# Extra ones products on TensorE in the first stage of a hybrid decoder block

## The chip, the cores and the metric

The kernel runs on one core of a Trainium2 chip. The metric is the time of one execution on the device in microseconds (us); a smaller time is better. Durations of single instructions come from one profiled execution of the program.

## The reference

One decoder layer over 1024 tokens of width 1024, all in float32. A conditioning vector `c` is turned into six modulation rows of 1024 (shift, scale and gate for each of two sub-layers):

```python
cond = jax.nn.silu(c)
mod = (cond @ w_ada[l] + b_ada[l]).astype(x.dtype)
sh_a, sc_a, gt_a, sh_m, sc_m, gt_m = [m[:, None, :] for m in jnp.split(mod, N_MOD, axis=-1)]
h = rms_norm(x, g_attn_pre[l]) * (1 + sc_a) + sh_a
proj = h @ w_in[l]
...
mixed = jnp.concatenate([rms_norm(oa, g_mix_a[l]), rms_norm(ob, g_mix_b[l])], axis=-1)
y = mixed @ w_out[l]
x = x + gt_a * rms_norm(y, g_attn_post[l])
h = rms_norm(x, g_mlp_pre[l]) * (1 + sc_m) + sh_m
y = jnp.square(jax.nn.relu(h @ w_up[l])) @ w_down[l]
x = x + gt_m * rms_norm(y, g_mlp_post[l])
```

`oa` is sliding-window attention with sinks over 8 heads, `ob` a mixture of dilated windows over 8 heads. Only the first lines, down to `proj`, matter for this change: the first two rows of `mod` must be known before the first projection can start.

## The kernel before

**Stages.** The program first loads `x` in eight blocks of 128 tokens (`x_sb`, tb 0 to 7) and the two needed thirds of `w_ada` in eight chunks (`wa`, k 0 to 7; each holds, for 128 output columns of the shift and 128 of the scale, all 1024 rows as 128 partitions by 8). Then come the input projection and attention, the output projection, and an MLP that takes most of the span. Float32 products are made of float32r pairs: a matrix is split into a high and a low part (`hw` for the activations, `w_hl` for the weights), and three products (lines 771, 772, 774) stand for one.

**The first stage.** For a block tb, ScalarE squares and sums (L553), VectorE and GpSimd make the root (L409, L412), VectorE scales the block (L558) and TensorE transposes it in two groups of four 128x128 transposes (L568) into PSUM tiles `pxt`, of which there are two. For tb 0 to 4 ScalarE copies them to `xnT` (L573). For tb 5 to 7 the copy out of PSUM also applies scale and shift (L580 on ScalarE or L583 on VectorE), and L593 and L596 split the block.

For a chunk k of `wa`, the product with `cond` is shared between two engines. TensorE takes the first two of the eight rows in one-column products (L615, the step `mod`; for k = 0 it takes all eight, 16 products); VectorE takes the other six: L626, then five times L628, into `acc_a`. VectorE adds TensorE's part to `bb` (L620) in between. A second pair of one-column products with `ones` (L635, the step `misc`) sums `acc_a` over the partitions into `pm`, and VectorE makes from that `g_a` and `s_a` of chunk k (L640, L641). Then ScalarE modulates chunk k of `xnT` (L645) and makes the high part (L651), GpSimd the low part (L654), and TensorE multiplies it with the k-th slice of the first weight unit: ten products of 384 columns for the five blocks (L771, L772), and later five more with the low part (L774). `w_hl` is made by L473 on ScalarE and L478 on GpSimd. The sums of the five blocks stand in five PSUM tiles `acc` of 512 columns, of which the products use 384. After the last chunk each block's `acc` is read out (`evac`: rotation L700 to L704, values L684 and L689, queries and keys L711 to L717), and the projection of block 5 (the same lines 771 to 774, with `pj` as output) waits for one of those tiles.

A product of float32 operands, such as L615 and L635, stands in the trace as two rows of TensorE; the transposes and the float32r products as one.

**What sets the order.** A planner in the program (`Sched`) has an estimated duration for every step and a clock for every engine, and writes the instructions out in the order in which the steps would start by these estimates. Each engine then executes its instructions strictly in that order; a wait in one holds up all that stand behind it. Steps of TensorE stand in streams (`xt` for the transposes, `mod`, `misc`, `dense` for the products, and others); steps of L580/L583, L593 and L596 may go to one of two engines, whichever the planner expects to end first.

Of the kernel before, what the change touches and what calls it, by code (L numbers as in the profile page):

```python
# [19 lines left out]
P = 128  # L20
# [114 lines left out]
class Sched:  # L135


    def __init__(self):
        self.clk = dict(PE=0.0, ACT=0.0, DVE=0.0, POOL=0.0, SP=0.0)
        self.queue = {e: [] for e in ("ACT", "DVE", "POOL", "SP")}  # L140
        self.pe = {}
        self.launch = []
        self.seq = 0
        self.dma = 0.0

    def step(self, dur, emit, deps=(), takes=(), gives=(), prio=5, after=None, kind=""):
# [83 lines left out]
    def run(self, prefer):  # L230
        while True:
# [28 lines left out]
            e, s, o, name = best  # L260
            if e == "PE":
                self.pe[name].pop(0)
            elif o.alts:
# [40 lines left out]
def hybrid_block(ctx: ExitStack, tc: tile.TileContext, x, positions, w_ada, b_ada, g_attn_post, w_in, w_out,  # L304
# [193 lines left out]

    e_init = op("DVE", 0.3, lambda: (V.memset(ones[:], 1.0), V.memset(nhalf[:], -0.5)), prio=0)
    e = op("ACT", 0.1, lambda: A.activation(cond[:], c_raw, AF.Exp, scale=-1.0), [e_c], prio=0)  # L500
# [49 lines left out]
    def x_block(tb):  # L550
# [13 lines left out]
        for g in range(2):  # L564
            def tr(g=g):
                box[g] = pt.tile([P, 4, P], F32, name="pxt", tag="t")
                for k in range(4):
                    T.transpose(box[g][:, k], x_t[tb][:, (4 * g + k) * P:(4 * g + k + 1) * P], ident)  # L568
            d = pe_op("xt", 0.7, tr, [e], takes=[(r_t, 1)], gives=[(r_x_, 1)] if g and tb < FIRST else [])
            d_all.append(d)  # L570
# [34 lines left out]
    def mod_chunk(k):  # L605
# [170 lines left out]
    def tick():  # L776
        st.d += 1 / (TB * KC)

    def first_unit():
        accs = {}  # L780
        for k in range(KC):
            for part in range(2):
                for tb in range(FIRST):
                    pl, tag, r = acc_at[tb]

                    def emit(k=k, part=part, tb=tb, pl=pl, tag=tag):
                        if k == 0 and part == 0:
                            accs[tb] = pl.tile([P, 512], F32, name="acc", tag=tag)
                        proj_mm(accs[tb][:, :UW], k, w_hl[0, k], tb, part)
                    d = dense(0.322 if part == 0 else 0.161, emit, [w_e[0, k], e_hl[k] if part else e_hh[k]],  # L790
                              takes=[(r, 1)] if k == 0 and part == 0 else [],
                              after=tick if part else None)
# [1157 lines left out]
```

## Time and profile before

| | |
|---|---|
| median of 3 runs | 1197.91 us (1197.79 to 1198.57) |
| profiled execution, its own time | 1197.14 us |
| its span | 1195.4 us |
| instructions | 17424 |
| TensorE busy in the span | 96% |
| VectorE, ScalarE, GpSimd busy | 74%, 56%, 22% |
| mean granted TensorE clock | 0.988 |

The profile is one execution on the chip. Its rows name the line of the kernel, the engine (PE is TensorE's products, PEld its weight loads, DVE VectorE, ACT ScalarE, POOL GpSimd, SP the engine that issues DMAs), the tile written and the tiles read. In the timeline, adjacent rows of one kind are merged: the first number is the start in us from the span's start, the second the time from the first start to the last end, `x8` the count, and in brackets stands the idle time ahead of it and what ended that. A busy TensorE can be one at half clock.

### The profile page before, as it was taken

How to read it: one execution, taken by the hardware profiler on the slowest of the kernel's cores; microseconds unless marked ns; L12 is line 12 of the kernel's file. 1: busy time of each engine (PE TensorE's matmuls, PEld its weight loads, DVE VectorE, ACT ScalarE, POOL GpSimd, SP SyncE). 2: the span in 40 equal slices, each digit the busy share in tenths (PEclk: the TensorE clock that was granted, in tenths of full speed). 3: DMA queues.
4: the chain of work that ended last, by engine and by line, in shares of the span. 5: the costliest groups of instructions: out<-in, count | busy, mean ns of one | idle time of the engine just before them, and what ended most of it. 6: DMA issues, size and time to landing. Idle time of an engine off the chain costs nothing.

```text
span 1195.4 us, 17424 instructions
## 1 busy us (share of the span) xinstructions
PE 1143.5 (96%) x6064; PEld 998.0 (83%) x6064; DVE 881.3 (74%) x1794; ACT 666.6 (56%) x1411; POOL 264.6 (22%) x325
## 2 busy tenths in 40 slices
PE   7879999999998998999899999999999999999996
PEld 6869999989998896888688888888888888888885
DVE  4977667666789897667888955479763797646998
ACT  6457666556666787667657533473325643246542
POOL 6534655465655333111100000000000000000002
PEclk9889999999999999999999999999999999999999
DMA  9621333213231422555296126952268511586103
GB/s 290 189 60 60 89 98 97 77 52 102 76 87 54 125 53 77 179 201 204 113 381 246 36 73 238 340 168 62 81 218 284 191 36 53 179 287 220 36 19 141
DMA packets 104423, 166.53 MB, mean 139 GB/s; under 512 B 11152, under 2 KB 56336, under 8 KB 104336
## 3 DMA queue, kind: packets, MB, share of 16 engines
q1 hardware_dynamic: 104336, 165.42, 41.8%
q8 instruction: 48, 0.79, 0.3%
q14 instruction: 39, 0.32, 0.1%
HBM read 137.08 MB, written 28.31 MB: 138 GB/s over the span
## 4 chain that ended last, share of the span: by engine, by line
PE 76%; DVE 13%; issue 4%; ACT 3%; POOL 3%; DMA 1%; SPq 0%; DVEq 0%; POOLq 0%; ACTq 0%
PE mlp_ps L1773 16%; PE mlp_ps L1774 16%; PE mlp_ps L1772 16%; PE pj L771 4%; PE pj L774 3%; PE pj L772 3%; PE s_ps L997 3%; PE o_ps L1131 1%; PE pt_ps L1100 1%; DVE acc_a L628 1%; PE y_ps L1348 1%; PE y_ps L1350 1%; PE pm L615 1%; PE y_ps L1349 1%; PE pt_ps L1103 1%
## 5 line engine op out<-in xcount | busy, mean ns | idle before, releaser
L1772 PE MATMUL mlp_ps<-hw 128*128 128x512 f32 x896 | 350.4, 391 | 0.4 <-ACT hw L1534 0.4
L1773 PE MATMUL mlp_ps<-hw 128*128 128x512 f32 x896 | 349.2, 390 | 1.1 <-DVE hw L1540 1.1
L1774 PE MATMUL mlp_ps<-hw 128*128 128x512 f32 x896 | 349.1, 390 | 0.0
L1773 PEld LDWEIGHTS mlp_ps<-hw 128*128 128x128 f32 x896 | 168.6, 188 | 36.9 <-DVE hw L1540 1.4
L1772 PEld LDWEIGHTS mlp_ps<-hw 128*128 128x128 f32 x896 | 168.6, 188 | 36.1 <-ACT hw L1534 0.8
L1774 PEld LDWEIGHTS mlp_ps<-hw 128*128 128x128 f32 x896 | 168.5, 188 | 35.1
L1543 DVE TENSOR_TENSOR hw<-w,hw 128x1024 fp32r<-128x1024 f32 x96 | 114.6, 1219 | 93.5 <-ACT hw L1536 93.3
L1536 ACT CAST hw<-w 128x1024 fp32r<-128x1024 f32 x96 | 97.4, 1046 | 129.9 <-PE mlp_ps L1774 93.2
L1872 POOL TENSOR_TENSOR st<-st,nhalf 128x1 f32<-128x1 f32 x8 | 7.8, 978 | 602.8 <-DVE st L1870 602.8
L771 PE MATMUL pj<-w_hl,hw 128*128 128x384 f32 x344 | 128.2, 373 | 10.0 <-DVE sk L717 10.0
L774 PE MATMUL pj<-w_hl,hw 128*128 128x384 f32 x344 | 117.4, 341 | 0.0
L772 PE MATMUL pj<-w_hl,hw 128*128 128x384 f32 x344 | 117.1, 341 | 0.0
L1536 ACT CAST hw<-u 128x1024 fp32r<-128x1024 f32 x48 | 48.6, 1051 | 64.6 <-PE mlp_ps L1774 64.6
L1118 DVE TENSOR_TENSOR ph<-pt_ps,ph 128x512 fp32r<-128x512 f32 (+1 forms) x110 | 68.8, 643 | 18.5 <-ACT ph L1114 17.6
L771 PEld LDWEIGHTS pj<-w_hl,hw 128*128 128x128 f32 x344 | 65.8, 191 | 11.8 <-issue 8.7
L1543 DVE TENSOR_TENSOR hw<-u,hw 128x1024 fp32r<-128x1024 f32 x48 | 57.0, 1217 | 18.2 <-ACT hw L1536 18.2
L1114 ACT CAST ph<-pt_ps 128x512 fp32r<-128x512 f32 (+1 forms) x110 | 59.2, 560 | 13.8 <-PE pt_ps L1103 9.8
L772 PEld LDWEIGHTS pj<-w_hl,hw 128*128 128x128 f32 x344 | 66.2, 192 | 0.8 <-issue 0.2
L774 PEld LDWEIGHTS pj<-w_hl,hw 128*128 128x128 f32 x344 | 65.7, 191 | 0.0
L1027 POOL TENSOR_SCALAR p_sb<-p_sb,den 128x128 f32<-128x128 f32 (+3 forms) x64 | 50.1, 786 | 70.2 <-DVE den L1025 46.8
L1830 DVE TENSOR_TENSOR yacc<-yacc,mlp_ps 128x512 f32<-128x512 f32 x96 | 62.1, 680 | 3.3 <-PE mlp_ps L1774 3.3
L1022 ACT ACTIVATE p_sb<-p_sb,mn 128x128 f32<-128x128 f32 (+3 forms) x64 | 49.9, 780 | 20.4 <-DVE mn L1015 16.6
(209 smaller groups left out, 2202.6 us busy)
## 6 DMA issues: line engine op xcount, KB each, us to landing
hw<-s_dram SPq DMA_DIRECT2D x84, 512.0 KB, 4.5
wa_st<-in_w_ada SPq DMA_DIRECT2D x32, 512.0 KB, 4.0
w<-in_w_up SPq DMA_DIRECT2D x32, 512.0 KB, 5.4
w<-in_w_down SPq DMA_DIRECT2D x32, 512.0 KB, 8.0
s_dram<-hw SPq DMA_DIRECT2D x28, 512.0 KB, 4.3
x_sb<-in_x SPq DMA_DIRECT2D x16, 512.0 KB, 6.2
wa<-in_w_ada SPq DMA_DIRECT2D x16, 512.0 KB, 7.0
w_st<-in_w_in SPq DMA_DIRECT2D x32, 192.0 KB, 4.7
```

The costliest lines, as they stand in the source:

```text
L771: T.matmul(ps, hw[:, tb, 0, t], w[:, 0], start=(k == 0), stop=False)
L772: T.matmul(ps, hw[:, tb, 0, t], w[:, 1], start=False, stop=False)
L774: T.matmul(ps, hw[:, tb, 1, t], w[:, 0], start=False, stop=(k == KC - 1))
L1027: lambda b=b, qi=qi: G.tensor_scalar(rec.p[qi], rec.p[qi], b["den"][:], 1.0, ALU.mult, ALU.mult), [e], prio=1))
L1114: A.copy(b["ph"][:, 0, :w], b["pt"][:, :w])
L1118: V.tensor_tensor(b["ph"][:, 1, :w], b["pt"][:, :w], b["ph"][:, 0, :w].bitcast(F32), ALU.subtract)
L1536: A.copy(out[j][0], flat(src[j]))
L1543: V.tensor_tensor(out[j][1], flat(src[j]), out[j][0].bitcast(F32), ALU.subtract)
L1772: T.matmul(ps[m][:], sh, mh, start=starts and k == 0, stop=False, **kw)
L1773: T.matmul(ps[m][:], sh, ml_, start=False, stop=False, **kw)
L1774: T.matmul(ps[m][:], sl, mh, start=False, stop=k == 3, **kw)
L1830: e = op("DVE", t_dv(512), lambda: V.tensor_tensor(y(), y(), ps[m][:], ALU.add), [e, ml.e_y[tb, n]], gives=gives, prio=1)
```

## The change

Four things change, all of them in the first stage.

1. Whenever the planner places a TensorE step, and until the first product of chunk 7 has been placed, it first calls `filler`. That emits groups of four 128x128 float32r products of a tile of ones with itself (L800 of the changed kernel) into columns 384 to 511 of the `acc` tile of block 4, which nothing reads before they are overwritten. There are as many groups as fit into the pause that the planner expects on TensorE at 0.24 us a group, and at least one ahead of each step that is not in the stream `dense`. They wait for nothing but the tile of ones. There are 336 such products.
2. VectorE makes the float32r tile of ones at the start (one more instruction).
3. The tile `acc` of block 4 is taken before the first product.
4. The planner's estimates of three steps change: a group of four transposes from 0.7 to 0.43 us, one row of `mod` from 0.426 to 0.224, the step `misc` from 0.43 to 0.23. This moves instructions on TensorE, VectorE, ScalarE and GpSimd within the first stage; the DMAs and everything after it keep their order.

```diff
+    ones_r = p0.tile([P, P], F32R, name="ones_r")
+    fill = Tok()
+    fill.open = False
+    def f_init():
+        V.memset(ones[:], 1.0)
+        V.tensor_copy(ones_r[:], ones[:])
+        V.memset(nhalf[:], -0.5)
+    e_init = op("DVE", 0.4, f_init, prio=0)
...
-            d = pe_op("xt", 0.7, tr, [e], takes=[(r_t, 1)], gives=[(r_x_, 1)] if g and tb < FIRST else [])
+            d = pe_op("xt", 0.43, tr, [e], takes=[(r_t, 1)], gives=[(r_x_, 1)] if g and tb < FIRST else [])
...
-            e = pe_op("mod", 0.426 * jp, pm0, [wa_e[k], e_cond], takes=[(r_x, 1)],
+            e = pe_op("mod", 0.224 * jp, pm0, [wa_e[k], e_cond], takes=[(r_x, 1)],
...
-            e = pe_op("misc", 0.43, pm, [e, e_init], takes=[(r_x, 1)], gives=[(r_acc, 1)])
+            e = pe_op("misc", 0.23, pm, [e, e_init], takes=[(r_x, 1)], gives=[(r_acc, 1)])
...
+    FILL, accs = 4, {}
+    def filler(start, name):
+        t = max(sc.clk["PE"], (e_init.t or start) + 0.2)
+        n = max(0, int((start - t - 0.06) / 0.24))
+        if e_init.t is not None and name != "dense":
+            n = max(n, 1)
+        for _ in range(4 * n):
+            T.matmul(accs[FILL][:, UW:], ones_r[:], ones_r[:], start=not fill.open, stop=not fill.open)
+    sc.filler = filler
...
+                        fill.open |= tb == FILL
+                        if k == KC - 1:
+                            sc.filler = None
```

On TensorE the program of before begins with the transposes of blocks 0 and 1, the 16 one-column products of chunk 0, more transposes and the first products of chunk 1:

```order
L568 MATMUL pxt<-head,x_sb 128x128 x12
L615 MATMUL pm<-cond,wa 128x1 x16
L568 MATMUL pxt<-head,x_sb 128x128 x20
L615 MATMUL pm<-cond,wa 128x1 x4
L568 MATMUL pxt<-head,x_sb 128x128 x8
L635 MATMUL pm<-ones,acc_a 128x1 x2
```

The changed program begins so (L580 are the transposes, L627 the one-column products, L800 the new ones):

```order
L800 MATMUL acc<-ones_r 128x128 x100
L580 MATMUL pxt<-head,x_sb 128x128 x4
L800 MATMUL acc<-ones_r 128x128 x4
L580 MATMUL pxt<-head,x_sb 128x128 x4
L800 MATMUL acc<-ones_r 128x128 x8
L580 MATMUL pxt<-head,x_sb 128x128 x4
L800 MATMUL acc<-ones_r 128x128 x4
L627 MATMUL pm<-cond,wa 128x1 x16
L800 MATMUL acc<-ones_r 128x128 x4
L580 MATMUL pxt<-head,x_sb 128x128 x4
L800 MATMUL acc<-ones_r 128x128 x32
L580 MATMUL pxt<-head,x_sb 128x128 x4
```

The transposes now stand in single groups with ones products between them. Further down on TensorE, before the sum of chunk 1 (L647):

```order
L800 MATMUL acc<-ones_r 128x128 x4
L580 MATMUL pxt<-head,x_sb 128x128 x4
L800 MATMUL acc<-ones_r 128x128 x4
L627 MATMUL pm<-cond,wa 128x1 x4
L800 MATMUL acc<-ones_r 128x128 x36
L647 MATMUL pm<-ones,acc_a 128x1 x2
L783 MATMUL acc<-w_hl,hw 128x384
```

All seven groups of transposes that are left after chunk 0 now stand ahead of chunk 1's products L627, where five of them did; with them stand 72 ones products, and 36 more ahead of L647.

On VectorE, after the last L628 of chunk 7, the program of before has this (L558 scales block 6 and then block 7, L640 and L641 belong to chunk 7, and L583 empties a `pxt` tile):

```order
L409 TENSOR_SCALAR rs_t<-ssq 128x1
L558 TENSOR_SCALAR x_sb<-x_sb,rstd 128x1024
L640 TENSOR_SCALAR g_a<-pm,bb,head 128x1
L641 TENSOR_SCALAR s_a<-pm,bb 128x1
L409 TENSOR_SCALAR rs_t<-ssq 128x1
L583 TENSOR_SCALAR x_sb<-pxt,g_a,s_a 128x128 x4
L558 TENSOR_SCALAR x_sb<-x_sb,rstd 128x1024
L593 CAST hw<-x_sb 128x1024
L596 TENSOR_TENSOR hw<-x_sb,hw 128x1024
L583 TENSOR_SCALAR x_sb<-pxt,g_a,s_a 128x128 x4
L593 CAST hw<-x_sb 128x1024
L583 TENSOR_SCALAR x_sb<-pxt,g_a,s_a 128x128 x4
```

And the changed program this:

```order
L412 TENSOR_SCALAR rs_t<-ssq 128x1
L652 TENSOR_SCALAR g_a<-pm,bb,head 128x1
L653 TENSOR_SCALAR s_a<-pm,bb 128x1
L570 TENSOR_SCALAR x_sb<-x_sb,rstd 128x1024
L595 TENSOR_SCALAR x_sb<-pxt,g_a,s_a 128x128 x4
L412 TENSOR_SCALAR rs_t<-ssq 128x1
L605 CAST hw<-x_sb 128x1024
L570 TENSOR_SCALAR x_sb<-x_sb,rstd 128x1024
L608 TENSOR_TENSOR hw<-x_sb,hw 128x1024
L712 TENSOR_TENSOR ra<-acc,cosw 128x64
L714 TENSOR_TENSOR acc<-acc,sinw 128x4x8 x2
L716 TENSOR_TENSOR acc<-ra,acc 128x4x16
```

`g_a` of chunk 7 moved ahead of the scaling of block 6, and the first rotation (L712) ahead of the casts of the last two blocks. One of VectorE's three groups that empty `pxt` is now ScalarE's. Besides, VectorE has `g_a` of chunks 1 and 3 straight behind the last L628 of their chunk, where L626 of the next chunk stood in between, and L620 one or two L628 earlier in chunks 4 to 7, and ahead of the angle steps (L534 to L537) in chunk 2.

More of the change, by code (lines that the diff above doesn't have):

```diff
@@ L144, in __init__ @@
         self.dma = 0.0
+        self.filler = None
     def step(self, dur, emit, deps=(), takes=(), gives=(), prio=5, after=None, kind=""):
@@ L261, in run @@
             if e == "PE":
+                if self.filler:
+                    self.filler(s, name)
                 self.pe[name].pop(0)
@@ L777, in tick @@
         st.d += 1 / (TB * KC)
+    FILL, accs = 4, {}
[7 more added lines that the diff above has]
+    sc.filler = filler
     def first_unit():
-        accs = {}
+        accs[FILL] = acc_at[FILL][0].tile([P, 512], F32, name="acc", tag=acc_at[FILL][1])
+        acc_at[FILL][2].free.pop()
         for k in range(KC):
@@ L786, in emit @@
                     def emit(k=k, part=part, tb=tb, pl=pl, tag=tag):
-                        if k == 0 and part == 0:
+                        if k == 0 and part == 0 and tb != FILL:
                             accs[tb] = pl.tile([P, 512], F32, name="acc", tag=tag)
+                        fill.open |= tb == FILL
+                        if k == KC - 1:
+                            sc.filler = None
                         proj_mm(accs[tb][:, :UW], k, w_hl[0, k], tb, part)
                     d = dense(0.322 if part == 0 else 0.161, emit, [w_e[0, k], e_hl[k] if part else e_hh[k]],
-                              takes=[(r, 1)] if k == 0 and part == 0 else [],
+                              takes=[(r, 1)] if k == 0 and part == 0 and tb != FILL else [],
                               after=tick if part else None)
```

1 line of the change is left out of this document (removed).

## The prediction

> **What bounds the kernel now.** I read the page's head first, then busy time by stretch, because the change ends when the first projection does.
>
> ```profile
> span 1195.4 us, 17424 instructions
> 7.50:20.70 13.20, 13.17 (x61) 12.36 (x62) 3.76 (x11) 7.32 (x13) 8.98 (x25) 1.00 1.11 322
> 33.00:60.90 27.90, 23.72 (x136) 22.44 (x135) 25.07 (x48) 12.75 (x21) 16.13 (x12) 0.88 0.59 169
> 60.90:77.20 16.30, 9.32 (x58) 8.48 (x58) 14.80 (x48) 8.09 (x28) 7.40 (x5) 0.89 0.35 101
> ```
>
> The columns after the length are the busy times of PE, PEld, DVE, ACT and POOL, the granted clock, and the DMA. TensorE is the full engine only in the first stretch. From 33 to 77.2 VectorE is busy 39.9 of 44.2 us, against TensorE's 33.0: the later part of the stage is a VectorE queue. The clock column says 1.00 for the first stretch, and the timeline of TensorE shows otherwise:
>
> ```profile
> 7.53 2.92 PE L568 MATMUL pxt<-head,x_sb 128*128 128x128 f32 x12 [7.53 <-DVE rs_t L409]
> 10.24 6.83 PE L615 MATMUL pm<-cond,wa 128*128 128x1 f32 x32
> 16.93 4.68 PE L568 MATMUL pxt<-head,x_sb 128*128 128x128 f32 x20
> 21.40 1.71 PE L615 MATMUL pm<-cond,wa 128*128 128x1 f32 x8
> 28.70 0.67 PE L771 MATMUL acc<-w_hl,hw 128*128 128x384 f32 x1
> 31.41 0.52 PE L771 MATMUL acc<-w_hl,hw 128*128 128x384 f32 x1
> 31.73 0.52 PE L772 MATMUL acc<-w_hl,hw 128*128 128x384 f32 x1
> 34.72 0.33 PE L772 MATMUL acc<-w_hl,hw 128*128 128x384 f32 x1
> 34.89 0.33 PE L771 MATMUL acc<-w_hl,hw 128*128 128x384 f32 x1
> 37.21 0.61 PE L635 MATMUL pm<-ones,acc_a 128*128 128x1 f32 x4 [1.46 <-DVE acc_a L628]
> 41.21 0.52 PE L772 MATMUL acc<-w_hl,hw 128*128 128x384 f32 x1
> 41.53 0.52 PE L771 MATMUL acc<-w_hl,hw 128*128 128x384 f32 x1
> 50.59 0.50 PE L635 MATMUL pm<-ones,acc_a 128*128 128x1 f32 x4
> 50.95 0.95 PE L774 MATMUL acc<-w_hl,hw 128*128 128x384 f32 x4
> 52.10 0.95 PE L615 MATMUL pm<-cond,wa 128*128 128x1 f32 x8
> 52.91 0.42 PE L771 MATMUL acc<-w_hl,hw 128*128 128x384 f32 x1
> 57.71 1.07 PE L568 MATMUL pxt<-head,x_sb 128*128 128x128 f32 x8
> 58.53 0.42 PE L771 MATMUL acc<-w_hl,hw 128*128 128x384 f32 x1
> ```
>
> Read start to start, a 384-column product takes 0.32 us at 31.4 and 41.2 but 0.17 at 34.7: half and full clock. The 11 us of transposes and one-column products from 10.24 on did not raise it, the dense products from 28.70 did, 3.0 to 5.8 us after their begin, and it was down again at 41.2. At half clock four transposes take 0.9 us (20 in 4.47, to the next row) and a one-column row 0.21; at full clock 0.41 and 0.10 ((58.53-57.71)/2, (52.91-52.10)/8). The step L635 takes 0.99 to 0.61 us against 0.36 (50.95-50.59); its row of 0.99 stands below. Now VectorE and GpSimd, and who waits at the end of the stage:
>
> ```profile
> 20.68 0.35 DVE L626 TENSOR_SCALAR acc_a<-wa,cond 128x256 f32<-128x256 f32 x1
> 21.06 1.68 DVE L628 SCALAR_TENSOR_TENSOR acc_a<-wa,cond,acc_a 128x256 f32<-128x256 f32 x2
> 23.14 0.16 DVE L620 TENSOR_TENSOR bb<-bb,pm 128x2 f32<-128x2 f32 x1 [0.40 <-PE pm L615]
> 23.21 2.14 DVE L628 SCALAR_TENSOR_TENSOR acc_a<-wa,cond,acc_a 128x256 f32<-128x256 f32 x3
> 25.50 0.99 PE L635 MATMUL pm<-ones,acc_a 128*128 128x1 f32 x4 [0.58 <-DVE acc_a L628]
> 26.52 0.28 DVE L640 TENSOR_SCALAR g_a<-pm,bb,head 128x1 f32<-128x1 f32 x1 [0.85 <-PE pm L635]
> 45.08 0.28 DVE L640 TENSOR_SCALAR g_a<-pm,bb,head 128x1 f32<-128x1 f32 x1 [0.76 <-PE pm L635]
> 50.69 0.48 DVE L628 SCALAR_TENSOR_TENSOR acc_a<-wa,cond,acc_a 128x256 f32<-128x256 f32 x1
> 58.07 2.83 DVE L628 SCALAR_TENSOR_TENSOR acc_a<-wa,cond,acc_a 128x256 f32<-128x256 f32 x3
> 58.53 1.57 POOL L654 TENSOR_TENSOR hw<-xnT,hw 128x640 fp32r<-128x640 f32 x1 [2.65 <-ACT hw L651]
> 61.63 0.75 DVE L558 TENSOR_SCALAR x_sb<-x_sb,rstd 128x1024 f32<-128x1024 f32 x1 [0.67 <-POOL rstd L412]
> 65.08 0.69 DVE L593 CAST hw<-x_sb 128x1024 fp32r<-128x1024 f32 x1 [0.38 <-ACT x_sb L580]
> 68.33 1.35 DVE L583 TENSOR_SCALAR x_sb<-pxt,g_a,s_a 128x128 f32<-128x128 f32 x4
> 77.18 0.66 PE L771 MATMUL pj<-w_hl,hw 128*128 128x384 f32 x1 [5.56 <-DVE sk L717]
> ```
>
> One L628 takes 0.48 us alone, three took 2.83 while GpSimd's L654 ran for 1.57: the two stand in each other's way, so their work adds up. VectorE waits for TensorE only in places, 0.40, 0.85 and 0.76 us. The stage ends at 77.18, when VectorE has emptied a block's sums. Whatever TensorE gains counts only through those waits.
>
> **The change part by part.** All sums are shifts against before; minus is earlier.
>
> *Price of a ones product.* No row shows one. Bounds come from rows that follow:
>
> ```profile
> 83.14 0.46 PE L736 MATMUL pk<-ident_r,sk 128*128 128x128 f32 x4
> 83.44 0.41 PE L771 MATMUL pj<-w_hl,hw 128*128 128x384 f32 x1
> ```
>
> Four float32r transposes of the same shape take 0.30, 0.075 each; a third of a 384-column product is 0.057. I take 0.067, twice that at half clock: a group of four is 0.27 or 0.54, where the planner has 0.24.
>
> *The early part, to L620 of chunk 1.* The first 100 products can start at about 1.2 us, when a first row of 0.17 and a copy are through (an estimate); no wait holds them. If the clock rises after 4 us (3.0 to 5.8 above), 30 run at half clock and 70 at full, 4.7 us: they end near 9.9, where the transposes had begun at 7.53. Three groups of transposes (1.23) and 16 more products (1.07) bring the 32 rows of chunk 0 to 12.2, which is two us later than before; they take 3.2 instead of 6.7 us. But they are a stretch without dense products as long as those after which the clock fell, so I add 1.0 (0 to 2): the end is at 16.4, where it was 16.93. Then stand seven groups of transposes, 2.9 us, and 72 ones products, 4.8 us, with another 1.0 at half clock: chunk 1's products begin at 25.1 instead of 21.40, take 0.8, and VectorE passes L620 at 26.1 instead of 23.14. That is +2.9. With a quick rise and no fall it is +0.4, with two falls +5. What hides it is little: VectorE has done all ahead of L620 by then, and the blocks' data (scaled by 20.7 in before) are there. The planner takes 1.79 us for chunk 0's products (8 x 0.224), half of what full clock gives, so its pauses are shorter in truth than it fills.
>
> Some comes back. While VectorE stands, GpSimd does its splits undisturbed; in the rows at 21.06 and 23.21, five L628 took 3.8 instead of 2.4 us, so I give back 1.5 (0.5 to 2). L635 of chunk 1 at full clock gives 0.6. Against that, L620 of chunk 2 now waits for L627 behind two pairs of products and a group: 0.7 + 0.27 + 0.81 against VectorE's 1.2, 0.5 more. Sum of the part: 2.9 - 1.5 - 0.6 + 0.5 = +1.3, between -0.8 and +4.
>
> *The middle, chunks 3 to 7.* L635 of chunks 3 and 4 at full clock saves 0.25 each (0.61 to 0.36). `g_a` of chunk 3 straight behind its sum makes VectorE stand 0.35 longer, since L626 no longer lies in that wait, and the earlier L620 of chunks 5 and 7 wait some 0.4 more in all. Ones products cost nothing here: VectorE is late, so TensorE runs them in pauses like the 1.46 us at 37.21; without that cover a group is 0.27. Sum +0.3, between -1 and +1.3.
>
> *The tail, from the last L628 to 77.18.* One of three L583 groups goes to ScalarE: -1.35. `g_a` fills half of the wait of 0.67 at 61.63: -0.3. The wait of 0.38 at 65.08 goes, since other work stands there: -0.35. ScalarE has room, 8.1 busy of 16.3. Sum -2.0, between -2.4 and -1.0. Next late are the two casts and `pj` itself, which finds TensorE at half clock after its idle 5.56, as before.
>
> *The rest.* VectorE's extra instruction lies ahead of its first wait. Behind 77.2 all queues are as they were, so the shift goes through.
>
> Sum: 1.3 + 0.3 - 2.0 = -0.4. The profiled execution took 1197.14, of which 1.74 lie outside the span; it is 0.77 under the median of 1197.91. So: profiled 1196.7, median 1197.5.
>
> The rows from 37.21 to 41.53 bear on one rule. TensorE had no idle time longer than 1.46 us there, and the clock fell nevertheless. The Trainium skill, "TensorE: Matmul & The Clock Gate", section "Why this matters for your kernels", says that gaps of over about 3 us let it fall. The trace does not agree that only these do. By that rule the fall during chunk 0's rows would not come, and the early part would be +1.3 less 2.0.
>
> **The rivals.** *The clock holds* (faster). Dense products ahead of and behind chunk 0's rows keep the clock up. Then L620 of chunk 1 is passed at about 23.5, the early part comes to -0.8, the middle, without a single fall, to -1, the tail to -2.2: -4.0, so 1193.9. For it: the fall at 41 came in a stretch with pauses, not in a full one. Against: 11 us of such rows never raised the clock.
>
> *The fillers hold up the transposes* (slower). TensorE's queue is in order; with a late rise and two falls L620 comes at 28, the early part is +4, the middle +1.3, the tail only -1.5: +3.8, so 1201.7. It decides from the point where L620 of chunk 1 is passed after about 27.5. For it: the 13.17 busy of 13.20 us in the first stretch leaves no pause in which to hide 72 products. Against: half of that stretch was half clock.
>
> *Ones products do not raise the clock at all* (the change does not do what it says). 100 at 0.134 are 13 us, chunk 0 ends at 26, chunk 1's products 16 us later, and L620 is at 44, +20; perhaps 4 come back: 1213 or more. Against it speaks that float32r products did raise it at 34.7.
>
> **How the numbers follow.** Forecast 0.55, clock holds 0.25, held-up transposes 0.15, no rise 0.05. A measurement of this kernel can tell about 0.2% from no change, 2.4 us: the forecast and what is near it count as same, 0.55; faster 0.25; slower 0.20. The range goes from the first rival's value, 1193.5, to the second's, 1202.0, and leaves out the third and the ends.
>
> **What would show it.** Right: 384-column products at 0.17 us from their first row on; transposes in groups of 0.41; the first transposes between 9 and 11 us; chunk 0's rows at 0.10 at first and perhaps 0.21 later; VectorE waiting at L620 of chunk 1 for L627 by several us; the last L628 ending within 2 us of 60.9; from there to the first `pj` 14.4 instead of 16.3 us. Wrong: L620 of chunk 1 well before 23, or a first stage that ends 3 us or more off 77.18, or a shift that is not kept to the end.

## The result and the profile after

| | before | change |
|---|---|---|
| median of 4 runs each, same chip | 1198.24 us (1197.79 to 1199.15) | 1235.98 us (1225.39 to 1243.69) |
| ratio, 95% interval | | 1.0308 [1.0222, 1.0394] |
| profiled execution | 1197.14 us | 1243.69 us |
| instructions | 17424 | 18100 |
| first `pj` | 77.18 us | 118.77 us |

The change is slower by 3%, some 38 us, where 1197.5 was forecast with a range to 1202.0. The profiled execution is the slowest of its four, so its shifts are somewhat larger than the medians' difference. In the changed kernel every line of the first stage stands 12 lines further down: L580 are the transposes, L627 the one-column products, L647 the sums over partitions, L638 and L640 VectorE's blends, L632 the addition to `bb`, L652 makes `g_a`. L800 are the ones products.

The timeline of TensorE, to be read start to start as before:

```profile
1.30 21.60 PE L800 MATMUL acc<-ones_r 128*128 128x128 f32 x100 [1.30 <-DVE ones_r L509]
22.69 1.07 PE L580 MATMUL pxt<-head,x_sb 128*128 128x128 f32 x4
...
28.41 6.93 PE L627 MATMUL pm<-cond,wa 128*128 128x1 f32 x32
35.20 1.09 PE L800 MATMUL acc<-ones_r 128*128 128x128 f32 x4
...
49.48 1.08 PE L580 MATMUL pxt<-head,x_sb 128*128 128x128 f32 x4
...
54.34 0.64 PE L580 MATMUL pxt<-head,x_sb 128*128 128x128 f32 x4
...
55.21 1.00 PE L627 MATMUL pm<-cond,wa 128*128 128x1 f32 x8
56.07 4.21 PE L800 MATMUL acc<-ones_r 128*128 128x128 f32 x36
60.12 0.55 PE L647 MATMUL pm<-ones,acc_a 128*128 128x1 f32 x4
...
89.81 4.36 PE L800 MATMUL acc<-ones_r 128*128 128x128 f32 x20
93.97 0.95 PE L647 MATMUL pm<-ones,acc_a 128*128 128x1 f32 x4
```

The first 100 products take 21.39 us, 0.214 each, from the first to the last: the clock does not rise in 21 us of ones products without a pause. The transposes, which began at 7.53, begin at 22.69, and chunk 0's rows run at 0.212 each (6.79 us for 32), as before. At full clock, from 56.07, a ones product takes 0.1125 us (4.05 for 36). From 89.81, 20 of them run at half clock again and do not raise it. A ones product costs what a one-column product costs, at either clock: 0.1125 beside 0.1075 (0.86 for 8 at 55.21), and 0.214 beside 0.212. Its 128 columns are not what is paid.

The clock first rises near 54.3: up to 53.45 four transposes still take 0.73 us and four ones products 0.89, at 54.34 and 54.73 only 0.39 and 0.48. No 384-column product has run yet (the first is at 60.54). What ran since 49.48 are groups of four transposes and of four ones products by turns. So 100 ones products alone did not raise the clock, and a mixture of them with transposes, which have 128 columns too, did.

The groups of TensorE's weight loads at full clock, first of the changed kernel between 55 and 60.5 us (count, busy time and mean in ns), show what a ones product and a one-column product have in common:

```profile
L800 PEld LDWEIGHTS acc<-ones_r 128*128 128x128 f32 x39 | 4.5, 192 | 0.0
L627 PEld LDWEIGHTS pm<-cond,wa 128*128 128x128 f32 x8 | 1.0, 192 | 0.0
```

and then, of before, the transposes from which the prediction took its price (minimum, median and maximum in ns):

```profile
L736 PEld LDWEIGHTS pk<-ident_r,sk x8: 138/142/223, 80.2 to 83.3; 128*128 128x128 f32 x8
```

A ones product has the load of a one-column product, 192 ns, not that of a transpose, 142. At half clock the load of a ones product takes 333 ns (mean from 1 to 22 us), longer than the 0.214 us that it costs, so loads overlap with the products ahead of them.

VectorE's timeline has long waits (three of chunk 1's blends follow the second of them):

```profile
35.37 0.28 DVE L652 TENSOR_SCALAR g_a<-pm,bb,head 128x1 f32<-128x1 f32 x1 [26.01 <-PE pm L627]
...
56.25 0.16 DVE L632 TENSOR_TENSOR bb<-bb,pm 128x2 f32<-128x2 f32 x1 [12.59 <-PE pm L627]
56.32 3.27 DVE L640 SCALAR_TENSOR_TENSOR acc_a<-wa,cond,acc_a 128x256 f32<-128x256 f32 x3
...
99.53 0.16 DVE L632 TENSOR_TENSOR bb<-bb,pm 128x2 f32<-128x2 f32 x1 [3.38 <-PE pm L627]
99.60 2.04 DVE L640 SCALAR_TENSOR_TENSOR acc_a<-wa,cond,acc_a 128x256 f32<-128x256 f32 x4
...
104.05 0.28 DVE L652 TENSOR_SCALAR g_a<-pm,bb,head 128x1 f32<-128x1 f32 x1 [2.35 <-PE pm L647]
```

and its three largest waits in the first 120 us, with total, count and longest, all end with TensorE:

```profile
DVE g_a L652 <- PE pm L627: 26.0, 1, 26.0
DVE bb L632 <- PE pm L627: 18.7, 6, 12.6
DVE g_a L652 <- PE pm L647: 9.3, 7, 2.3
```

The stage's shift divides at two points. The addition of chunk 1's rows comes at 56.25 instead of 23.14: +33.1. From there to the end of the last blend are 45.4 us (to 101.64) instead of 37.8 (23.14 to 60.90): +7.6. From there to the first `pj` are 17.1 instead of 16.3: +0.8. Together +41.6, and behind the first `pj` the order is as before. Of the 33.1, the first transposes account for 15.2 (22.69 instead of 7.53). The other 18.0 come between them and the addition, where 88 more ones products stand in the queue: at 0.214 each they are some 18.8 us.

### The profile page after: what moved, and what is told of

It reads as the page before. It is cut to its first block, busy times and chain, and to the rows that moved or that the text cites. A ratio compares the mean times of both kernels' runs of the same rounds, so it can differ in the third digit from the quotient of the medians.

```text
span 1241.9 us, 18100 instructions
## 1 busy us (share of the span) xinstructions
PE 1199.4 (97%) x6400; PEld 1056.0 (85%) x6400; DVE 877.2 (71%) x1791; ACT 668.2 (54%) x1415; POOL 262.9 (21%) x325
## 4 chain that ended last, share of the span: by engine, by line
PE 78%; DVE 11%; ACT 4%; issue 3%; POOL 2%; DMA 2%; SPq 0%; DVEq 0%; POOLq 0%; ACTq 0%
PE mlp_ps L1802 15%; PE mlp_ps L1803 15%; PE mlp_ps L1801 15%; PE acc L800 5%; PE pj L783 4%; PE pj L786 3%; PE pj L784 3%; PE s_ps L1026 2%; PE o_ps L1160 1%; PE pt_ps L1129 1%; PE pm L627 1%; PE y_ps L1377 1%; PE y_ps L1379 1%; PE y_ps L1378 1%; PE pt_ps L1132 1%
## 5 line engine op out<-in xcount | busy, mean ns | idle before, releaser
L800 PE MATMUL acc<-ones_r 128*128 128x128 f32 x336 | 63.9, 361 | 1.3 <-DVE ones_r L509 1.3
```

The source lines that it names most:

```text
L800: T.matmul(accs[FILL][:, UW:], ones_r[:], ones_r[:], start=not fill.open, stop=not fill.open)
```

## The experiments

Theory W, formed on this trace: a ones product is bounded by its weight load, and because its 128 columns stream in only half of that time (0.057 of 0.1125 us, an estimate by a third of a 384-column product at 0.17), products of this width never raise the clock. So the products only delay. Further rivals are stated with the runs that they belong to. Rival P: the planner's new order does the damage. Rival D: products of ones with ones do not raise the clock because their data never change. In the kernels with wider ones products all lines move by three more: L583 are the transposes, L630 the one-column products, L650 the sums, L635 the addition to `bb`, L641 and L643 the blends, L655 `g_a`, L573 the scaling. "Against before" is always the kernel before on the same chip.

**The order alone.** No ones products, the change's estimates.

```diff
-    sc.filler = filler
+    sc.filler = None
```

> The changed kernel without any ones product, with the new estimates and so the new order of all other instructions. Theory W (the ones products cost the time: each is as long as its weight load, 0.21 us at half clock and 0.11 at full, and a 128-column product keeps the array streaming only half of that, too little to raise the clock): without them the first projection of block 5 starts between 74 and 77 us (77.2 before, 118.8 in the change), and the time is 1195 to 1199 us. Rival P (the new order costs the time, since the planner takes half of the true time for the one-column products): 1220 us or more, with L620's wait of over 10 us still there.

Measured: 1203.78 us against 1199.57 before, ratio 1.0026 [1.0009, 1.0043]. Neither theory had it, and `pj` comes at 82.78 where W had 74 to 77: the order is not the bulk of the loss, but it is not the small gain that W took over from the prediction either. Of VectorE in this run:

```profile
17.86 0.28 DVE L652 TENSOR_SCALAR g_a<-pm,bb,head 128x1 f32<-128x1 f32 x1 [7.89 <-PE pm L627]
...
18.99 0.80 DVE L570 TENSOR_SCALAR x_sb<-x_sb,rstd 128x1024 f32<-128x1024 f32 x1 [0.67 <-POOL rstd L415]
...
23.88 0.35 DVE L638 TENSOR_SCALAR acc_a<-wa,cond 128x256 f32<-128x256 f32 x1
```

`g_a` of chunk 0 now stands ahead of the scaling of block 2 as well (before, only of blocks 3 and 4), which so starts at 18.99 instead of 13.62, and chunk 1's first blend at 23.88 instead of 20.68. The last blend ends at 67.69 instead of 60.90, and the first `pj` is at 82.78: the tail is 15.1 us instead of 16.3, so of the 2.0 us forecast for the tail 1.2 are there.

**Ones products of 512 columns.** Ahead of block 4's first real product each group of four becomes one product of 512 columns.

```diff
-        for _ in range(4 * n):
-            T.matmul(accs[FILL][:, UW:], ones_r[:], ones_r[:], start=not fill.open, stop=not fill.open)
+        for _ in range(4 * n if fill.open else n):
+            if fill.open:
+                T.matmul(accs[FILL][:, UW:], ones_r[:], ones_r[:], start=False, stop=False)
+            else:
+                T.matmul(accs[FILL][:], ones_r[:], ones_w[:], start=True, stop=True)
```

> Until the first real product, each group of four 128-column ones products is one product of 512 columns; the data are still ones. Theory W: a 512-column product streams almost all of its time, so the clock rises 3 to 6 us after the first one; 0.43 us each until then, 0.22 afterwards; first transposes at 8 to 10 us, first 384-column products at 0.17 us, total 1194 to 1204 us. Rival D (the clock counts switching, and products of ones do not switch): no rise, 0.43 us each, first transposes at 12 us, total 1210 us or more.

Measured: 1204.59 us against 1199.57, ratio 1.0058 [1.0035, 1.0081]. TensorE's timeline:

```profile
1.84 7.64 PE L806 MATMUL acc<-ones_w,ones_r 128*128 128x512 f32 x25 [1.84 <-DVE ones_w L512]
9.32 0.60 PE L583 MATMUL pxt<-head,x_sb 128*128 128x128 f32 x4
...
11.58 3.63 PE L630 MATMUL pm<-cond,wa 128*128 128x1 f32 x32
15.07 0.48 PE L806 MATMUL acc<-ones_w,ones_r 128*128 128x512 f32 x1
...
15.76 3.64 PE L806 MATMUL acc<-ones_w,ones_r 128*128 128x512 f32 x8
19.24 0.60 PE L583 MATMUL pxt<-head,x_sb 128*128 128x128 f32 x4
```

Here the clock rises: 25 products in 7.48 us, which at 0.43 and 0.227 (estimates, four thirds of 0.32 and 0.17) is some 9 at half clock and the rest at full, so some 4 us after their start. The transposes begin at 9.32 and chunk 0's rows run from 11.58 to 15.07 at 0.109 each, close to the 9.9 and the 12.2 to 16.4 of the prediction's early part. After the rows the clock falls: eight products take 3.48 us. This is the nearest to the change as it was meant, and it is still slower than before, half a microsecond above W's range. It has the new order, which alone cost 4.2 us, and behind block 4's first real product still groups of 128 columns. Its profiled execution, 1214.20 us, is the slowest of its ten, so its later rows show more delay than the median has.

**Ones products of 256 columns**, in the same number.

```diff
+                T.matmul(accs[FILL][:, 256:], ones_r[:], ones_w[:], start=True, stop=True)
```

> Until the first real product each ones product has 256 columns instead of 128, their number is the same. Theory W: the price stays that of the weight load, 0.21 us at half clock and 0.11 at full, although twice the columns are streamed, and the clock rises 3 to 6 us after the first one, so the 100 end near 14.5 us instead of 22.7; total about 1205 to 1215 us. Rival C (the price is by columns): 0.43 and 0.21 us each. Rival D (ones do not count for the clock): 0.21 us each all the time, the first transposes at 22.7 us, total as the change, 1225 to 1244.

Measured, one execution: 1219.83 us.

```profile
1.57 14.43 PE L806 MATMUL acc<-ones_w,ones_r 128*128 128x256 f32 x100 [1.57 <-DVE ones_w L512]
15.83 0.60 PE L583 MATMUL pxt<-head,x_sb 128*128 128x128 f32 x4
```

100 products of twice the columns end at 15.8, almost seven us earlier than those of 128. In the trace they begin 0.214 us apart for the first 4.9 us and 0.12 apart behind that: some 23 ran at half clock and 77 at full. Twice the columns cost no more at half clock and little more at full, and the wider ones of the same data raise the clock. That refutes D. W had the 100 end near 14.5 and at most 1215 us: although the clock rises, the run still loses 20 us.

**Other data.** The 128-column products multiply a piece of `x` with itself.

```diff
-        V.tensor_copy(ones_r[:], ones[:])
+    e_init = op("DVE", 0.2, lambda: V.tensor_copy(ones_r[:], x_t[0][:, 0:P]), [x_e[0]], prio=-1)
```

> The 128-column products multiply a 128x128 piece of x instead of ones; as many as in the change, but they can start only when x has landed, near 5.5 us. Theory W: 0.21 us each, no rise of the clock while they run alone, the 100 end near 27 us, total 1228 to 1250 us. Rival D: with random data the clock rises 3 to 6 us after the first one, 0.11 us each from then on, the 100 end near 18 us, total 1205 to 1220 us.

Measured, one execution: 1251.16 us; the products start only when `x` is there.

```profile
6.20 21.60 PE L801 MATMUL acc<-ones_r 128*128 128x128 f32 x100 [6.20 <-DVE ones_r L511]
27.60 1.08 PE L580 MATMUL pxt<-head,x_sb 128*128 128x128 f32 x4
```

0.214 each, no rise: in these 100 products the data make no difference. The time is 1 us above W's range.

**192 columns.**

```diff
+                T.matmul(accs[FILL][:, 320:], ones_r[:], ones_w[:], start=True, stop=True)
```

> The change with 192 columns in each ones product ahead of block 4's first real product (the same number of products). Theory W: a product still takes its weight load's time, 0.113 us at full clock or 0.214 at half, because 192 columns stream in 0.085 and 0.16 or so; the columns fill three quarters of it, between the half of 128 columns, which never raised the clock, and the whole of 256, which raised it at about 6.8 us. If the clock goes by the share of time in which columns stream with a limit under three quarters, the 100 products end between 14 and 18 us and the run takes 1215 to 1228 us; if the limit is above, they take 21.4 us at 0.214 and the run takes 1230 to 1250 us. Rival T (any gap between two products' columns keeps the clock down): 21.4 us, 1230 to 1250 us.

Measured, one execution: 1220.49 us.

```profile
1.54 13.23 PE L806 MATMUL acc<-ones_w,ones_r 128*128 128x192 f32 x100 [1.54 <-DVE ones_w L512]
14.60 0.60 PE L583 MATMUL pxt<-head,x_sb 128*128 128x128 f32 x4
```

13.06 us for 100: some 17 at half clock and 83 at full, a rise 3.7 us after the start. Ones products whose columns fill three quarters of the 0.214 us raise the clock, those whose columns fill half of it do not (estimates, from 0.32 us for 384 columns at half clock); a gap in each product is no bar. Where between 128 and 192 columns the limit lies was not tried. That the share of time is what counts is argued, not shown: the transposes further down do not fit it as it stands.

**Waking without the new order.** The estimates of before, and 16 products of 512 columns ahead of the first transposes, no others.

```diff
+        n = 0 if fill.first else 16
+        fill.first = True
+        for _ in range(n):
+            T.matmul(accs[FILL][:], ones_r[:], ones_w[:], start=True, stop=True)
```

> As the run with the hold, but only the 16 ones products of 512 columns ahead of the first transposes; the rest of every engine's order is that of before. Theory W: the clock rises near 6 us, the rows of chunk 0 take 0.11 us each, the clock falls again after them between 14 and 19 us as it did in the run with groups of 512 columns, so chunk 1's rows take 0.21 again; the last blend 0 to 1.5 us earlier than 60.90; 1196 to 1199.5 us. Rival V: within 0.5 us of before, 1198.5 to 1200.5 us. Rival Q: 16 products end by 8.5 us, so 0 to 1 us slower than before, not over 1201 us.

Measured: 1197.28 us against 1199.18, ratio 0.9986 [0.9970, 1.0001]. On TensorE and then on VectorE:

```profile
1.84 6.37 PE L801 MATMUL acc<-ones_w,ones_r 128*128 128x512 f32 x16 [1.84 <-DVE ones_w L512]
...
9.97 3.63 PE L630 MATMUL pm<-cond,wa 128*128 128x1 f32 x32
13.46 0.68 PE L583 MATMUL pxt<-head,x_sb 128*128 128x128 f32 x4
...
16.43 2.91 PE L583 MATMUL pxt<-head,x_sb 128*128 128x128 f32 x12 [0.28 <-ACT xnT L588]
...
74.93 0.66 PE L786 MATMUL pj<-w_hl,hw 128*128 128x384 f32 x1 [5.54 <-DVE sk L732]
```

```profile
14.13 0.80 DVE L573 TENSOR_SCALAR x_sb<-x_sb,rstd 128x1024 f32<-128x1024 f32 x1 [0.67 <-POOL rstd L415]
14.85 0.27 DVE L655 TENSOR_SCALAR g_a<-pm,bb,head 128x1 f32<-128x1 f32 x1
...
55.84 2.82 DVE L643 SCALAR_TENSOR_TENSOR acc_a<-wa,cond,acc_a 128x256 f32<-128x256 f32 x3
```

Chunk 0's rows end at 13.46, 3.5 us earlier; `g_a` comes only 2.25 us earlier, since it now waits behind the scaling of block 2; the last blend ends at 58.66 and `pj` comes at 74.93, both 2.2 us earlier. The clock falls again after the rows (12 transposes take 2.91 us from 16.43). The stage ends earlier than W had it (at most 1.5 us), and the time lies in W's range; V, by which VectorE alone sets the stage's end, is wrong in this trace. The time over five rounds gains 0.14%, but its interval reaches no change, so a gain in time is not shown.

**Waking and holding.** The same, with one product of 512 columns ahead of each transpose step, row group and sum.

```diff
+        if not fill.open and name != "dense":
+            n = 1 if fill.first else 16
```

> The planner's estimates are those of before, so VectorE's and ScalarE's order is that of before; 16 ones products of 512 columns stand ahead of the first transposes and one of 512 columns ahead of each transpose step, row group and sum until the first real product of block 4; none of 128 columns. Theory W (a 128-column ones product is bounded by its weight load, fills half of that time with columns and never raises the clock; the change's loss is 21 us of such products at half clock plus some 3 us of the order): the clock rises near 6 us, the rows of chunk 0 take 0.11 us each instead of 0.21 and end near 13.6 instead of 17.07, the addition of chunk 1's rows (23.14 before) comes 1 to 3 us earlier, the last blend 0 to 2 us earlier than 60.90; 1195 to 1199 us. Rival V (VectorE's order and its own work set the stage's end, TensorE's clock does not): the rows come earlier but the last blend ends within 0.5 us of 60.90; 1198.5 to 1200.5 us, the same as before. Rival Q (any ones product in TensorE's queue delays the blends behind it, whatever its width): over 1202 us.

Measured: 1197.85 us against 1199.18, ratio 0.9998 [0.9977, 1.0019]. TensorE after chunk 0's rows:

```profile
15.93 0.78 PE L803 MATMUL acc<-ones_w,ones_r 128*128 128x512 f32 x1
16.73 1.12 PE L583 MATMUL pxt<-head,x_sb 128*128 128x128 f32 x4
...
19.88 0.95 PE L630 MATMUL pm<-cond,wa 128*128 128x1 f32 x8
```

The single products do not hold the clock through the rows and the waits behind them: at 15.93 it is at half again. It is up once more for chunk 1's rows (0.81 us for 8, to the next row at 20.69). The last blend ends at 58.96 and `pj` is at 75.23, no better than without them: a fast chunk 1 gained nothing. Q, that any product in the queue costs, is wrong at this number and width.

**Waking with the new order.** As the waking run, with the change's estimates.

```diff
-            e = pe_op("mod", 0.426 * jp, pm0, [wa_e[k], e_cond], takes=[(r_x, 1)],
+            e = pe_op("mod", 0.224 * jp, pm0, [wa_e[k], e_cond], takes=[(r_x, 1)],
```

The estimates of `xt` and `misc` are those of the change as well.

> The 16 ones products of 512 columns ahead of the first transposes, none else, with the change's estimates and so its order. Theory W with the order's price explained by the clock (the order cost 4 us without ones products because chunk 0's sums waited for rows at half clock and stood ahead of three blocks' scaling): with the rows at 0.11 us each chunk 0's g_a comes near 14.5 instead of 17.86, the scaling of block 2 near 15.5 instead of 18.99, the last blend near 59 to 62, the tail 15.1 as in the run without ones products; 1194 to 1198.5 us, no slower than the run with before's estimates (1197.28). Rival O (the order itself costs its 4 us whatever the clock, since the scaling of blocks 2 to 4 stands behind the sums): the last blend 63 us or later; 1199.5 to 1203 us.

Measured: 1201.06 us against 1199.36, ratio 1.0019 [1.0003, 1.0035]. Rival O holds: the order costs some 3.6 us beside the run with before's estimates (+1.7 against -1.9, each against before on its own chip), though chunk 0's `g_a` came at 13.74 and block 2's scaling at 14.88. The tail is 15.1 again, and the last blend ends at 63.02 instead of 58.66. VectorE's waits for TensorE from 12 to 62 us say where that comes from; of this run:

```profile
DVE bb L635 <- PE pm L630: 5.0, 6, 1.7
DVE g_a L655 <- PE pm L630: 4.5, 1, 4.5
DVE g_a L655 <- PE pm L650: 3.6, 5, 1.1
```

and of the run with before's estimates:

```profile
DVE g_a L655 <- PE pm L650: 2.0, 3, 0.8
DVE bb L635 <- PE pm L630: 0.7, 1, 0.7
```

The 4.5 us are the wait of chunk 0's `g_a`, ahead of block 2. They cost little: block 2's scaling is only 0.75 us later than in the other run (14.88 and 14.13). The rest is 8.6 us of waits instead of 2.7. The estimates of full clock put the additions and `g_a` earlier into VectorE's queue than TensorE delivers, and the blends that used to stand ahead of them no longer cover those waits.

This run also has a row on the clock. It falls after chunk 0's rows; then, on TensorE:

```profile
15.82 5.64 PE L583 MATMUL pxt<-head,x_sb 128*128 128x128 f32 x24 [1.62 <-DVE x_sb L573]
21.28 0.97 PE L630 MATMUL pm<-cond,wa 128*128 128x1 f32 x8
```

24 transposes take 5.46 us, with two short pauses; in a row they begin 0.21 us apart, which is half clock. Behind them eight one-column rows end within 0.97 us, which is full clock. So transposes of 128 columns did raise it, where 100 ones products of 128 columns did not. In before, 20 of them in 4.47 us had not. What sets transposes apart stays open: at half clock their load is shorter (220 ns in the mean against 333), their price is the same.

**One group a step.** The change with no pause filled: n = 0, so one group of four ahead of each step that is not `dense`.

```diff
-        n = max(0, int((start - t - 0.06) / 0.24))
+        n = 0
```

> The change without the ones products that fill pauses: only the one group of four 128-column products that stands ahead of each step (24 groups until block 4's first real product, some more behind it), with the change's estimates and order. Theory W: the first group costs 0.86 us in a pause, the later ones 0.43 to 0.86 us each in TensorE's queue, beside the order's 3 us of the run without ones products (1203.8); the clock is half until real products of 384 columns stand in a row; 1204 to 1214 us. Rival G (only the 100 products ahead of the first transposes cost anything, the groups between them hide in waits): 1202.5 to 1205 us, within 1.5 us of the run without ones products. Rival Q (the groups in the queue are the main cost): over 1214 us.

Measured: 1211.88 us against 1199.18, ratio 1.0094 [1.0062, 1.0127]: 8.5 us over the order alone (+12.7 and +4.2, on two chips). W's range held. G, by which groups between the steps hide in waits, is wrong.

**The first 100 alone.** Before's estimates, and only the 100 products of 128 columns ahead of the first transposes.

```diff
+        n = 0 if fill.first else 100
+        fill.first = True
+        for _ in range(n):
+            T.matmul(accs[FILL][:, UW:], ones_r[:], ones_r[:], start=True, stop=True)
```

> Only the 100 ones products of 128 columns ahead of the first transposes, no group after them, before's estimates. Theory W: 21.4 us at 0.214, the first transposes at 22.7 instead of 7.53, so 15 us late; VectorE and the transfers had waits of 2 to 3 us there that take up a little of it; the last blend 10 to 15 us later than 60.90; 1208 to 1214 us, so about a third of the change's 38 us, and the rest is the groups and pauses behind it. Rival A (the first 100 are nearly the whole loss): 1225 to 1236 us. Rival S (the slack of the later stages takes most of it up): under 1205 us.

Measured: 1215.86 us against 1199.36, ratio 1.0137 [1.0118, 1.0155], some 2 us more than W had. The first transposes are at 22.69 and

```profile
92.27 0.66 PE L783 MATMUL pj<-w_hl,hw 128*128 128x384 f32 x1 [5.56 <-DVE sk L729]
```

the first `pj` comes 15.1 us late: of a delay of 15.2 at the start the stage gives nothing back.

**All products, before's estimates.** The three estimates of the change are set back, that of `mod` among them; the planner then finds pauses for 240 ones products instead of 336.

```diff
-            e = pe_op("mod", 0.224 * jp, pm0, [wa_e[k], e_cond], takes=[(r_x, 1)],
+            e = pe_op("mod", 0.426 * jp, pm0, [wa_e[k], e_cond], takes=[(r_x, 1)],
```

> The change with its ones products as they are, but the planner's estimates of before, so the order of VectorE is that of before; 100 products of 128 columns ahead of the first transposes. Additive theory W: the products cost what they cost and the order's 4 us go; 1227 to 1235 us. Rival M (the planner's order and the products hinder each other, so that the order was the larger part): under 1220 us. Rival N (the order costs nothing beside the products): 1235 to 1244 us.

Measured: 1223.60 us against 1199.36, ratio 1.0203 [1.0180, 1.0225], between W's range and M's. With ones products in the pauses the new estimates cost 13.5 us (37.7 less 24.2), without them 4.2. The 96 products more that they call for are part of that; how large a part was not separated, and the change's own time is known only to some 10 us either way (ratio 1.0222 to 1.0394).

**No later pauses.** The change, but behind the first 100 never more than one group.

```diff
-            n = max(n, 1)
+            n = 1 if fill.first else n
+            fill.first = True
+        if name == "dense":
+            n = 0
```

> The change with its order, the 100 ones products ahead of the first transposes and one group of four ahead of each later step, but no more than one group in the later pauses: 212 products instead of 336. Additive theory W (order 4.2 us, one group a step 8.1, the first 100 some 15 to 16.5, the 124 products of the later pauses the rest of the change's 38 us): 1226 to 1230 us. Rival I (the first 100 and the new order hinder each other, the later pauses hide in waits): 1233 to 1239 us, as the change. Rival L (the later pauses are over half of what is left, and part of the 100 is hidden by the new order's waits): 1217 to 1225 us.

Measured: 1227.81 us against 1197.96, ratio 1.0236 [1.0211, 1.0261], as W said. On TensorE the first 100 products leave the clock at half once more, but three groups of transposes and ones products by turns, from 22.69 on, raise it for chunk 0's rows:

```profile
27.55 3.81 PE L627 MATMUL pm<-cond,wa 128*128 128x1 f32 x32
```

They take 0.115 each (3.68 us, to the next row at 31.23), where the change, with eight ones products in one of these groups, had 0.212.

So the change's 37.7 us add up along these kernels, each against before on its own chip: the order 4.2, one group a step 8.5 more, the first 100 products 17.2 more (to 29.9), the 124 products of the later pauses 7.8 more. The last term is the least certain: the change's four executions go from 1225.39 to 1243.69 us, the fastest of them below this run. The split also depends on the order in which the parts are added.

## Why the prediction was wrong

Two steps of the early part failed, the price of a ones product and the rise of the clock; a third, that ones products cost nothing in the middle, failed with them.

*Price of a ones product.* This step failed. 0.067 us was taken from transposes and from a third of a 384-column product; measured are 0.1125 at full clock and 0.214 at half, outside the bounds 0.057 to 0.075. The right row stood in the prediction: a one-column product at 0.10 and 0.21 (and the first stage's own transposes, 0.41 for four at full clock). The one-column product, too, has a whole 128x128 weight load for little streaming, and its load lasts as long as a ones product's. That the load, and not another fixed cost of each product, sets the price is inferred; the runs show that the price is the same for 1, 128 and 192 columns. The Trainium skill, "TensorE: Matmul & The Clock Gate", section "LDWEIGHTS (loading the stationary operand)", puts a load at the number of columns over 1.2 in ns, 107 for 128. A product's measured 112.5 at full clock is close to that, its 214 at half clock and the loads' own rows, 192 and 333, are not.

*The early part.* The step "if the clock rises after 4 us" failed. Of the loss of 38 us it carried nearly half: in the runs with 192 and 256 columns the clock rose, and they still lost 21 and 20 us (one execution each) to the price, the order and the products in the queue. The step was taken from 384-column products and handed on to products of 128 columns. With products of 192, 256 and 512 columns the rise came 3.7, 4.9 and some 4 us after their start; with 128 it did not come in 21. The same page, section "What's actually happening", has the clock rise after about 3.4 us of activity, after some 49 products of 128 columns; here 100 float32r products of that width did not do it, so for this kind the measurement decides. The addition of chunk 1's rows was forecast 2.9 us late and came 33.1 late. "What hides it is little" was right, and more so than meant: the run with the first 100 alone gave back nothing of 15.2. The 1.5 us that undisturbed blends were to give back did not come: chunk 1's five took 1.00 and 3.27 us in the change, 4.3 instead of 3.8, since the last three ran only after the long wait, when GpSimd had its splits again (L666 from 57.68 for 1.64 us).

In that part a second step failed by itself: that the new order is free up to there because "VectorE has done all ahead of L620 by then". It overlooked that `g_a` of chunk 0 now stands ahead of the scaling of block 2 too on VectorE, not only of blocks 3 and 4, so that TensorE's lateness at chunk 0 holds up the blocks and with them the transposes and the ones products behind these. Shown by the run of the order alone, 5.4 us at block 2.

*The middle.* "Ones products cost nothing here" failed. From the addition of chunk 1 to the last blend the forecast is +0.3 with the -1.5, -0.6 and +0.5 that the early part has behind that point, together -1.3; measured is +7.6. VectorE is not late once the first part has made TensorE late: the additions wait up to 3.38 us for rows that stand behind groups, and the 20 products at 89.81 run at half clock. One group a step cost 8.5 us over the stage. The small term for the earlier places of `g_a` and the additions, some 0.8 us, was too small: in the pair of waking runs the waits grew by 5.9 us and the last blend came 4.4 us later.

*The tail.* The mechanism was right and the size off: -1.2 instead of -2.0 in both runs with the new order and no later ones products. In the change itself it became +0.8, mostly because `g_a` of chunk 7 waits 2.35 us for its sum, where it waits 0.70 in both of those runs.

*The rest*, that the shift is kept to the end, held in the main: 41.6 of the 46.5 us that the profiled execution lost are there at the first `pj`. Where the other 4.9 came from was not followed.

*The rivals.* The mechanism of the third, that ones products do not raise the clock at all, is the one that happened to the first 100 and up to 54 us; it had a chance of 0.05 and 1213 us or more, and its price of 0.134 made that too small: 21.4 us instead of 13 for the first 100, and the addition of chunk 1 at 56 instead of 44. What spoke against it, "float32r products did raise it at 34.7", spoke of products that stream three times as long for one load. The 11 us of transposes and one-column products that had not raised the clock, quoted in the first part, were the nearer row, though transposes alone later did raise it. The ends of the range, 1193.5 and 1202.0, are not quite the two rivals' own 1193.9 and 1201.7; nothing hangs on that. Of the second rival, that fillers hold up the transposes, the mechanism is there too, at a much larger price.

The idea behind the change may be sound in a small form. An awake clock for chunk 0's rows brought the stage's end 2.2 us forward in the trace of the waking run; a gain in the time is not shown. The first 100 products of 128 columns alone cost 16.5 us.

## What to carry to other kernels

Price a short product by the row of a product that loads as much and streams as little, not by a share of a long one; and to wake a clock use wide products (192 columns and more did it here), and end them before the first real work arrives. An estimate in a planner is not only a duration: it moves instructions on every engine, and one that promises a late producer earlier than it delivers puts the waits into the queue of the consumer. Try the order without the products and the products without the order; here the first cost 4 us and the second, with 240 products, 24; together, with 336, they cost 38.

## What the runs showed of the hardware

TensorE can be busy in every row of the trace for 21 us and stay at half clock. For ones products in a row, each with a weight load, the width counted: 100 of 128 columns did not raise the clock, with ones or with other data, and those of 192 columns raised it in some 4 us. By 0.32 us for 384 columns, that is 50% and 75% of 0.214 us (estimates). The width is not the whole of it: 24 transposes of 128 columns in 5.46 us raised it in the run with waking and the new order, and groups of transposes and ones products by turns did in the change. At full clock a 192-column product costs what one of 128 columns costs, 0.113 us (4.08 for 36, from 34.65 in its run), one of a single column 0.1075, one of 256 columns 0.12. The granted clock in the stretches is no help at the start of this program: between 7.5 and 33 us of the changed kernel it says 1.00, where every product ran at half, and still 1.00 up to the rise near 54.3:

```profile
7.50:20.70 13.20, 13.20 (x64) 13.20 (x64) 0.94 (x3) 0.00 (x0) 4.35 (x14) 1.00 1.11 324
20.70:33.00 12.30, 12.30 (x61) 12.30 (x61) 0.00 (x0) 2.81 (x5) 0.00 (x0) 1.00 0.63 157
```

The durations say it, read start to start.
